# Two blocks of a transformer on one core: where the state-space Gelu and the poles' setup stand in the program

## The chip, the cores and the metric

The kernel runs on one core of a Trainium2 chip. The metric is the device time of one launch in microseconds. A core has TensorE (PE; its weight loads are PEld), VectorE (DVE), ScalarE (ACT), GpSimd (POOL) and the queue engine SyncE (SP). Each works through its own queue in the order in which the program puts the instructions there.

## The reference

x is 512 tokens of 1024 values, all in float32. The first block runs two layers of

```python
x = x + 0.5 * swiglu(rmsnorm(x, g_ffn1[l]), w_ffn1_gate[l], w_ffn1_up[l], w_ffn1_down[l])
...
x = x + merged @ w_out[l]
x = x + 0.5 * swiglu(rmsnorm(x, g_ffn2[l]), w_ffn2_gate[l], w_ffn2_up[l], w_ffn2_down[l])
```

The second block has an even layer (stick-breaking attention of 8 heads beside a state-space mixer) and an odd one (gated linear attention). What the change touches is the even layer:

```python
q = rms_norm(q.reshape(bsz, L, SB_HEADS, SB_HEAD_DIM), sb_q_norm_g[i])
k = rms_norm(k.reshape(bsz, L, SB_HEADS, SB_HEAD_DIM), sb_k_norm_g[i])
o_a = stick_breaking_attention(q, k, v).reshape(bsz, L, SB_WIDTH) * jax.nn.silu(z_a)
o_b = s5_mixer(u, ...) * jax.nn.silu(z_b)
```

`s5_mixer` makes complex poles and input weights from its parameters (`lam_bar = exp(lam * dt)`, `b_bar = (lam_bar - 1) / lam * b`), scans over time, and ends with `y = gelu(y)` and a gate `y * sigmoid(y @ w_glu + b_glu)`.

## The kernel before

Every large product is three matmuls (`mm3`, lines 200 to 202): both operands are split into a high and a low part. ScalarE copies the high part of a weight chunk (tile `wh`, line 111), VectorE subtracts to get the low part (`wl`, line 112). Two buffers each of `wr`, `wh` and `wl` hold the chunks, so a split waits until PE is done with the chunk before the last. A pool of 32 wide buffers (`g`) holds most intermediates, 8 PSUM banks (`b`) the products. The program is written in one order, and a scheduler places the instructions on each engine's queue at build time; what it chose is fixed.

The even layer (`even`, from line 1357) works in rounds c = 0 to 4. In a round below 4, PE makes q, k and v of heads 2c and 2c+1 in halves of two token tiles (`qk_half`, `form_b_pair`). ScalarE copies each half out of PSUM with the token scale `rce` and squares it; after the second half, VectorE, GpSimd (a power) and VectorE again make the norm's scale and multiply q or k (line 247); PE then turns them by transposes (`qk_turn`, line 269). Beside that, a round takes the two heads of the round before through `logits` (three banks; on ScalarE copies, Abs, Exp, Ln; on VectorE a maximum; on GpSimd a triangular mask, line 1259), `sums` (running sums by matmuls with constant triangles, lines 205), `values` and `gated`, with a unit of z by `silu_unit` for each. `ha` is the first of these heads, `hb` the second.

The state-space part runs one quarter of its groups a round: `states(c)` (matmuls 64 wide, a scan on VectorE), `outputs(c)` (matmuls into one bank, a copy by ScalarE, a store `s_ys` by SP's queue), `fed` and `load` (SP's queue fetches the next quarter's inputs `s_us` and tables), and `finish(c - 1)`: eight loads of the stored outputs by SP's queue, then the Gelu, which is an addition on VectorE, a Square on ScalarE, two operations on VectorE, a Tanh on ScalarE and two more on VectorE. Before the change `finish` stands behind `logits(ha)`.

A feed-forward (`ffn`, line 365) goes through its hidden units in thirds of 8, 8 and 6 chunks; each third ends with a down projection of four columns. The list `extra` hangs a step behind each of the first six half columns of every third's down projection. In the first feed-forward of layer 0 the poles' setup (`s5_setup`, some 60 short operations on VectorE, a chain of powers on GpSimd, two loads of b by ScalarE's queue) hangs in the last third, and `s5_keep`, which stores three results by GpSimd's queue, on the step behind it.

Of the kernel before, what the change touches and what calls it, by code (L numbers as in the profile page):

```python
# [50 lines left out]
class Kern:  # L51
# [851 lines left out]
    def s5_setup(self):  # L903

        nc, ins = self.nc, self.ins
# [3 lines left out]
        def A(n, w=16):  # L909
            i = 1 if n in ("s5th", "s5kk", "s5t2") else 0 if n in ("s5cn", "s5sn") else 2  # L910
            if i == 2:
                return self.tiny(w)
            used[i] += w
            return (keep, work)[i][:, used[i] - w:used[i]]
# [18 lines left out]
        t2, s, c = A("s5t2", W), A("s5s", W), A("s5c", W)  # L933
# [14 lines left out]
        nr, ni, t, u, den = A("s5nr"), A("s5ni"), A("s5t"), A("s5u"), A("s5den")  # L948
# [13 lines left out]
        self.tt(u, nr, im, ALU.mult)  # L962
        self.tt(t, t, u, ALU.subtract)
        self.tt(ci, t, den, ALU.mult)
        br, bi, t1, t2 = self.g()[:, 0:256], self.g()[:, 0:256], self.g()[:, 0:256], self.g()[:, 0:256]
        nc.scalar.dma_start(br, ins["s5_b_re"])
        nc.scalar.dma_start(bi, ins["s5_b_im"])
        v = lambda a: a.rearrange("p (j c) -> p j c", c=16)
        wide = lambda a: a.rearrange("p (j c) -> p j c", c=1).to_broadcast([P, 16, 16])
        both = self.g()  # L970
# [16 lines left out]
        for n in (1, 2, 4):  # L987
            a, b = slice(1, n + 1), slice(n + 1, 2 * n + 1)
            cr, ci = (t[:, n:n + 1, :].to_broadcast([P, n, 16]) for t in (lr, li))
            t = self.g()  # L990
            t1, t2 = (t[:, i * 64:i * 64 + n * 16].rearrange("p (k j) -> p k j", j=16) for i in range(2))
# [359 lines left out]
    def even(self):  # L1351
        nc, ins = self.nc, self.ins
        w_in = ins["even_w_in"]
        gf = self.par["g_final"]
        gg = self.const([P, KD], "gg")
        self.tt(gg, gf, self.par["even_norm_g_2"], ALU.mult)

        us, ys, oa, heads, sz = [], [], [], {}, {}
        load, feed, fed, states, outputs, finish = self.s5_steps(us, ys)
        xs = self.norm_start(gg)  # L1360
        w = self.weights(w_in[16])
        acc, acc2 = self.squares(), self.squares(gf)
        b = [self.form_a(w, 0, xs), self.form_a(w, 1, xs)]
        r1 = self.rms(self.col_sums(acc), 4, D, EPS)
        w = self.weights(w_in[17])
        b.append(self.form_a(w, 0, xs))
        ssf = self.tiny(4)
        self.tt(ssf, self.col_sums(acc2), r1, ALU.mult)
        self.tt(ssf, ssf, r1, ALU.mult)
        rcol = self.const([P, 4], "rce")  # L1370
        self.tt(rcol, self.rms(ssf, 4, D, EPS), r1, ALU.mult)
        b.append(self.form_a(w, 1, xs))
        d1, d2 = self.diag(r1), self.diag(rcol)
        R, R1 = self.rows(rcol, d2), self.rows(r1, d1)
        for i in range(4):
            u = self.g()
            self.tt(u, b[i], R, ALU.mult)
            us.append(u)
            feed(i)
        fed(0)  # L1380
        load(0)
        logits, sums, values, gated = self.sb_steps(heads, oa)

        def silu_unit(w, j):
            b = self.form_a(w, j, xs)
            s = self.g()
            self.tt(s, b, R, ALU.mult)
            self.act(s, s, AF.Silu)
            return s

        ob_s = []
        for c in range(5):
            ha, hb, hp = 2 * c - 2, 2 * c - 1, 2 * c - 3
            q, k = {}, {}
            if c < 4:
                w = self.weights(w_in[c])
                self.qk_half(w, 0, xs, rcol, q)
            else:
                wz = self.weights(w_in[18])
                ob_s.append(silu_unit(wz, 0))  # L1400
            if c > 1:
                values(hp)
                gated(hp, sz.pop(hp))
            if c > 0:
                logits(ha)
                finish(c - 1)
            if c < 4:
                self.qk_half(w, 2, xs, rcol, q)
                w = self.weights(w_in[4 + c])
                self.qk_half(w, 0, xs, rcol, k)  # L1410
                states(c)
            else:
                ob_s.append(silu_unit(wz, 1))
                wz = self.weights(w_in[19])
                ob_s.append(silu_unit(wz, 0))
                yp = [self.split(y) for y in ys]
            if 0 < c < 4:
                with self.tc.issue_after(q["rms"].ins):
                    sums(ha)
            elif c > 0:  # L1420
                sums(ha)
            if c < 4:
                self.qk_half(w, 2, xs, rcol, k)
                w = self.weights(w_in[8 + c])
                v2 = [self.g(), self.g()]
                qT = self.qk_turn(q, self.par["sb_q_norm_g_2"], P ** -0.5)
                self.form_b_pair(w, 0, xs, rcol, lambda i: v2[0][:, i * 256:(i + 1) * 256])
            else:
                ob_s.append(silu_unit(wz, 1))
            if c > 0:  # L1430
                values(ha)
            if c < 4:
                self.form_b_pair(w, 2, xs, rcol, lambda i: v2[1][:, i * 256:(i + 1) * 256])
                kT = self.qk_turn(k, self.par["sb_k_norm_g_2"], 1.0)
                for i in range(2):
                    heads[2 * c + i] = (qT[i], kT[i], [v2[t // 2][:, (t % 2) * 256 + i * P:(t % 2) * 256 + (i + 1) * P]
                                                       for t in range(4)])
            if c > 0:
                logits(hb)
                wz = self.weights(w_in[12 + c - 1])  # L1440
                sz[ha] = silu_unit(wz, 0)
                gated(ha, sz.pop(ha))
            if c < 4:
                outputs(c)
                if c < 3:
                    fed(c + 1)
                    load(c + 1)
            if c > 0:
                sz[hb] = silu_unit(wz, 1)
                if c < 4:  # L1450
                    sums(hb)
            if c == 1:
                for k in range(KD):
                    self.stt(self.x[k], self.x[k], gf[:, k:k + 1], R1, ALU.mult, ALU.mult)
        ob = []
        os_ = [self.split(o) for o in oa[:4]]
        for c in range(2):
            w = self.weights(ins["s5_w_glu"][c])
            for j in range(2):
                n = 2 * c + j  # L1460
                b = self.form_a(w, j, yp)
                th = self.g()
                self.act(th, b, AF.Tanh, scale=0.5, bias=self.bglu[:, n:n + 1])
                self.stt(th, th, 1.0, ys[n], ALU.add, ALU.mult)
                self.stt(th, th, 0.5, ob_s[n], ALU.mult, ALU.mult)
                ob.append(self.split(th, *(self.sp.tile([P, S], F32R, tag=t, name=self.nm(t), bufs=KD) for t in ("xh", "xl"))))
        os_ += [self.split(o) for o in oa[4:]] + [None] + ob
        banks, ws = [], {}

        def part(n, ks, first, last):  # L1470
            if n % 2 == 0 and first:
                ws[n // 2] = [self.weights(ins["even_w_out"][n // 2], k, 6) for k in (6, 0)][::-1]
            if first:
                banks.append(self.bank())
            js = slice((n % 2) * P, (n % 2 + 1) * P)
            for k in ks:
                w = ws[n // 2][k // 6]
                self.mm3(banks[n], (w[0][:, k % 6, js], w[1][:, k % 6, js]), os_[k], first and k == ks[0],
                         last and k == ks[-1])

        sums(7)
        ks = [8, 9, 10, 11, 0, 1, 2, 3, 4, 5, 6]
        part(0, ks, True, False)
        values(7)
        gated(7, sz.pop(7))
        os_[7] = self.split(oa[7])
        part(1, ks, True, False)
        for n in range(KD):
            part(n, [7] if n < 2 else ks + [7], n >= 2, True)
            self.tt(self.x[n], banks[n], self.x[n], ALU.add)  # L1490
# [222 lines left out]
def build(tc, ins, out, upto=99, first=0):  # L1713
    with ExitStack() as ctx:
        K = Kern(ctx, tc, ins, out)
        K.setup()
        idle = [nothing] * 6
        extras = [[[K.bias_loads, K.biases] + idle[2:] + idle + [K.s5_setup, K.s5_keep],
                   idle + K.s5_quad(0) + K.s5_quad(1)],
                  [idle + K.s5_quad(2) + K.s5_quad(3), idle + K.s5_tables(0) + [nothing] + K.s5_tables(1)]]  # L1720
        for l in range(DEPTH if first == 0 else 0):
# [120 lines left out]
```

## Time and profile before

| | us |
|---|---|
| median of three runs | 3108.08 (3104.66 to 3109.74) |
| the profiled execution | 3108.96 |
| its span, first to last instruction | 3107.1 |
| PE busy | 3044.2 |
| VectorE busy | 2039.7 |
| ScalarE busy | 1354.2 |
| GpSimd busy | 166.8 |

Times in the rows are microseconds from the span's start. A line ("L269") is that of the kernel; where a helper issues an operation, the line is the helper's and the tiles tell which step it is. PEclk is the granted share of TensorE's full clock: 1 is 2.4 GHz, half of it 1.2 GHz. The rounds of the even layer lie between about 2450 and 2810, the first feed-forward between 0 and 363.

### The profile page before, as it was taken

The numbers are of one execution on the slowest core, as the hardware profiler recorded it, in microseconds if no ns is written. First come the engines' busy times: TensorE is split into PE (matmuls) and PEld (weight loads), VectorE is DVE, ScalarE is ACT, GpSimd is POOL, SyncE is SP. The second block draws the span as 40 slices with busy tenths as digits, with TensorE's granted clock in tenths as the row PEclk, the third lists the DMA queues.
The fourth block names the chain that finished last, engine by engine and source line by source line (L and its number), as shares of the span: only waits on it lengthen the run. The fifth ranks groups of instructions, "written<-read, shape, count | busy, mean of one in ns | idle before, by whom it ended". The sixth has DMA issues, their size and how long they took to land. (4 is left out here: it accounts for less than half of the span.)

```text
span 3107.1 us, 44082 instructions
## 1 busy us (share of the span) xinstructions
PE 3044.2 (98%) x17718; PEld 2653.8 (85%) x17718; DVE 2039.7 (66%) x3630; ACT 1354.2 (44%) x2351; POOL 166.8 (5%) x308
## 2 busy tenths in 40 slices
PE   9999999999999999999999999999999988899999
PEld 7898888889888988898989889888989977777887
DVE  7787845655667887888864655558878644454643
ACT  5343335543443434443434553344434455463532
POOL 1000200000000011001010000000000010010010
PEclk9999999999999999999999999999999998899999
DMA  4332333322222333323343322222233331212211
GB/s 152 101 109 91 117 106 115 112 83 82 98 92 96 111 116 123 107 95 120 104 141 106 114 92 82 95 95 96 96 117 102 131 116 59 71 63 69 105 68 55
DMA packets 73548, 311.13 MB, mean 100 GB/s; under 512 B 18836, under 2 KB 20820, under 8 KB 44800
## 3 DMA queue, kind: packets, MB, share of 16 engines
q1 hardware_dynamic: 59680, 282.39, 26.4%
q10 hardware_dynamic: 9584, 16.74, 1.9%
q0 software_dynamic: 4080, 9.20, 1.2%
q8 instruction: 139, 2.28, 0.3%
q14 instruction: 65, 0.53, 0.1%
HBM read 292.48 MB, written 12.66 MB: 98 GB/s over the span
## 5 line engine op out<-in xcount | busy, mean ns | idle before, releaser
L200 PE MATMUL b<-xh,wh 128*128 128x512 f32 (+1 forms) x1880 | 693.7, 369 | 7.4 <-ACT xh L253 6.7
L202 PE MATMUL b<-xh,wl 128*128 128x512 f32 (+1 forms) x1880 | 684.4, 364 | 4.0 <-DVE wl L112 3.6
L201 PE MATMUL b<-xl,wh 128*128 128x512 f32 (+1 forms) x1880 | 683.8, 364 | 1.3 <-DVE xl L97 1.3
L111 ACT ACTIVATE wh<-wr 128x1024 fp32r<-128x1024 f32 (+2 forms) x396 | 383.0, 1004 | 582.8 <-PE b L201 347.7
L112 DVE TENSOR_TENSOR wl<-wr,wh 128x1024 fp32r<-128x1024 f32 (+2 forms) x396 | 453.1, 1162 | 154.7 <-ACT wh L111 152.9
L202 PE MATMUL b<-g,wl 128*128 128x512 f32 x1168 | 461.6, 395 | 1.2 <-DVE wl L112 1.2
L200 PE MATMUL b<-g,wh 128*128 128x512 f32 x1168 | 462.8, 396 | 0.0
L201 PE MATMUL b<-g,wh 128*128 128x512 f32 x1168 | 461.1, 395 | 1.5 <-DVE g L97 1.5
L200 PEld LDWEIGHTS b<-xh,wh 128*128 128x128 f32 x1880 | 356.5, 190 | 62.8 <-ACT xh L253 6.7
L202 PEld LDWEIGHTS b<-xh,wl 128*128 128x128 f32 x1880 | 356.1, 189 | 61.3 <-DVE wl L112 4.7
L201 PEld LDWEIGHTS b<-xl,wh 128*128 128x128 f32 x1880 | 356.4, 190 | 57.4 <-issue 2.1
L243 DVE TENSOR_TENSOR g<-b,g 128x512 f32<-128x512 f32 (+2 forms) x265 | 183.9, 699 | 254.0 <-PE b L202 238.9
L202 PEld LDWEIGHTS b<-g,wl 128*128 128x128 f32 x1168 | 220.0, 188 | 52.9 <-DVE wl L112 1.6
L201 PEld LDWEIGHTS b<-g,wh 128*128 128x128 f32 x1168 | 220.0, 188 | 52.5 <-DVE g L97 2.3
L200 PEld LDWEIGHTS b<-g,wh 128*128 128x128 f32 x1168 | 220.2, 189 | 52.0 <-issue 2.0
L200 PE MATMUL b<-wh,xh 128*128 128x256 f32 x896 | 259.5, 290 | 0.0
L201 PE MATMUL b<-wl,xh 128*128 128x256 f32 x896 | 256.4, 286 | 1.1 <-DVE wl L112 1.1
L202 PE MATMUL b<-wh,xl 128*128 128x256 f32 x896 | 255.7, 285 | 0.0
L243 DVE TENSOR_TENSOR g<-g,g 128x512 f32<-128x512 f32 (+8 forms) x373 | 201.8, 570 | 66.8 <-ACT g L253 62.4
L243 DVE TENSOR_TENSOR g<-g,b 128x256 f32<-128x256 f32 (+1 forms) x484 | 177.0, 397 | 29.1 <-PE b L202 25.2
L96 ACT ACTIVATE sw<-s 128x512 fp32r<-128x512 f32 x180 | 111.8, 630 | 191.9 <-DVE s L243 158.5
L253 ACT ACTIVATE g<-g 128x512 f32<-128x512 f32 (+4 forms) x280 | 143.6, 528 | 102.3 <-DVE g L243 86.1
(240 smaller groups left out, 5114.3 us busy)
## 6 DMA issues: line engine op xcount, KB each, us to landing
wr<-in_w_ffn_up SPq DMA_DIRECT2D x44, 1024.0 KB, 4.8
wr<-in_w_ffn_gate SPq DMA_DIRECT2D x43, 1024.0 KB, 4.8
wr<-in_w_ffn_down SPq DMA_DIRECT2D x32, 1024.0 KB, 4.9
wr<-in_w_gate SPq DMA_DIRECT2D x24, 1024.0 KB, 4.8
wr<-in_w_in SPq DMA_DIRECT2D x20, 1024.0 KB, 4.8
wr<-in_even_w_in SPq DMA_DIRECT2D x20, 1024.0 KB, 5.0
wr<-in_w_ffn_down SPq DMA_DIRECT2D x16, 768.0 KB, 4.2
g<-tb ACTq DMA_DIRECT2D x48, 256.0 KB, 3.0
```

The lines of the kernel that those rows point to most:

```text
L96: self.nc.scalar.activation(hi, src, AF.Copy)
L111: nc.scalar.activation(hi[:, :, js], raw[:, :, js], AF.Copy)
L112: nc.vector.tensor_tensor(out=lo[:, :, js], in0=raw[:, :, js], in1=hi.bitcast(F32)[:, :, js], op=ALU.subtract)
L200: t.matmul(out, l[0], r[0], start=start, stop=False)
L201: t.matmul(out, l[0], r[1], start=False, stop=False)
L202: t.matmul(out, l[1], r[0], start=False, stop=stop)
L243: return (eng or self.nc.vector).tensor_tensor(out=out, in0=a, in1=b, op=op)
L253: self.nc.scalar.activation(out, a, f, **kw)
```

## The change

It moves `finish(c - 1)` in rounds 1 to 3 from behind `logits(ha)` to the end of the round, behind `gated(ha)` and ahead of `outputs(c)`; in round 4 it stays. It moves `s5_setup` and `s5_keep` from the last third of the first feed-forward to the middle third, with one empty step between them. The loads of b go by GpSimd's queue, and four half-used wide buffers become two.

```diff
--- before.py
+++ after.py
@@ -962,9 +962,9 @@
         self.tt(u, nr, im, ALU.mult)
         self.tt(t, t, u, ALU.subtract)
         self.tt(ci, t, den, ALU.mult)
-        br, bi, t1, t2 = self.g()[:, 0:256], self.g()[:, 0:256], self.g()[:, 0:256], self.g()[:, 0:256]
-        nc.scalar.dma_start(br, ins["s5_b_re"])
-        nc.scalar.dma_start(bi, ins["s5_b_im"])
+        (br, bi), (t1, t2) = ((t[:, 0:256], t[:, 256:512]) for t in (self.g(), self.g()))
+        nc.gpsimd.dma_start(br, ins["s5_b_re"])
+        nc.gpsimd.dma_start(bi, ins["s5_b_im"])
         v = lambda a: a.rearrange("p (j c) -> p j c", c=16)
         wide = lambda a: a.rearrange("p (j c) -> p j c", c=1).to_broadcast([P, 16, 16])
         both = self.g()
@@ -1403,7 +1403,8 @@
                 gated(hp, sz.pop(hp))
             if c > 0:
                 logits(ha)
-                finish(c - 1)
+                if c == 4:
+                    finish(3)
             if c < 4:
                 self.qk_half(w, 2, xs, rcol, q)
                 w = self.weights(w_in[4 + c])
@@ -1440,6 +1441,8 @@
                 wz = self.weights(w_in[12 + c - 1])
                 sz[ha] = silu_unit(wz, 0)
                 gated(ha, sz.pop(ha))
+            if 0 < c < 4:
+                finish(c - 1)
             if c < 4:
                 outputs(c)
                 if c < 3:
@@ -1715,7 +1718,7 @@
         K = Kern(ctx, tc, ins, out)
         K.setup()
         idle = [nothing] * 6
-        extras = [[[K.bias_loads, K.biases] + idle[2:] + idle + [K.s5_setup, K.s5_keep],
+        extras = [[[K.bias_loads, K.biases] + idle[2:] + [K.s5_setup, nothing, K.s5_keep],
                    idle + K.s5_quad(0) + K.s5_quad(1)],
                   [idle + K.s5_quad(2) + K.s5_quad(3), idle + K.s5_tables(0) + [nothing] + K.s5_tables(1)]]
         for l in range(DEPTH if first == 0 else 0):
```

Three places in ScalarE's queue show what the scheduler makes of it. In the rows, `sb` tiles of 1280 columns are the logits' work buffers, `g<-b,rce` copies half of q, k or v out of PSUM, `g,y<-g` squares it, `wh<-wr` splits a weight chunk, and a `g<-g` of 512 columns is a Square, Tanh or Silu.

Round 1, from the two copies behind the mask on. Before:

```order
L253 ACTIVATE g_23508<-sb_23495 128x128
L253 ACTIVATE g_23507<-sb_23495 128x128
L111 ACTIVATE wh_23975<-wr_23973 128x8x128 x2
L253 ACTIVATE g_23523<-g_23522 128x512
L253 ACT_TABLE_LOAD
L253 ACTIVATE g_23524<-g_23523 128x512
L253 ACTIVATE g_23429<-b_23533,rce 128x256 x2
L253 ACTIVATE g_23532,y_23430<-g_23429 128x128 x4
L253 ACTIVATE g_23608<-b_23612,rce 128x256 x2
L253 ACTIVATE g_23611,y_23610<-g_23608 128x128 x4
```

Now:

```order
L253 ACTIVATE g_23506<-sb_23493 128x128
L253 ACTIVATE g_23505<-sb_23493 128x128
L253 ACTIVATE g_23427<-b_23512,rce 128x256 x2
L253 ACTIVATE g_23511,y_23428<-g_23427 128x128 x4
L253 ACTIVATE g_23587<-b_23591,rce 128x256 x2
L253 ACTIVATE g_23590,y_23589<-g_23587 128x128 x4
L253 ACT_TABLE_LOAD
L253 ACTIVATE sb_23492<-sb_23492 128x1280
L111 ACTIVATE wh_23954<-wr_23952 128x8x128
L253 ACTIVATE g_23588<-b_23712,rce 128x256 x2
L253 ACTIVATE g_23711,y_23589<-g_23588 128x128 x4
L111 ACTIVATE wh_23954<-wr_23952 128x8x128
```

The weight split (of z's chunk), Square, table load and Tanh stood ahead of the copies of q's second half and k's first; now those copies follow at once, the Exp of the sums behind them, and the split comes in two halves around the copies of k's second half.

The end of round 1 and the start of round 2, before; the first row copies the state outputs out of PSUM:

```order
L253 ACTIVATE g_24027<-b_24010 128x512
L253 ACT_TABLE_LOAD
L253 ACTIVATE g_24006<-g_24006 128x512
L111 ACTIVATE wh_24309<-wr_24307 128x8x128 x2
L253 ACT_TABLE_LOAD
L253 ACTIVATE sb_23954<-sb_23954 128x1280
L253 ACTIVATE sb_24201<-b_24194 128x512
L253 ACTIVATE sb_24201<-b_24196 128x256
L253 ACTIVATE sb_24201<-b_24195 128x512
L253 ACTIVATE g_24042<-s_r_3452 128x4x63 x2
L253 ACT_TABLE_LOAD
L253 ACTIVATE g_24082<-g_24082 128x512
```

Now, from the table load ahead of the Exp of the sums of `hb`:

```order
L253 ACT_TABLE_LOAD
L253 ACTIVATE sb_23933<-sb_23933 128x1280
L253 ACTIVATE g_23999<-g_23998 128x512
L253 ACTIVATE g_24000<-g_23999 128x512
L253 ACTIVATE g_24025<-b_24008 128x512
L253 ACTIVATE sb_24199<-b_24192 128x512
L253 ACTIVATE sb_24199<-b_24194 128x256
L253 ACTIVATE sb_24199<-b_24193 128x512
L253 ACTIVATE sb_24200<-sb_24199 128x1280
L253 ACTIVATE sb_24200<-sb_24200 128x1280
L253 ACT_TABLE_LOAD
L253 ACTIVATE sb_24200<-sb_24200 128x1280
```

Square, Tanh and the copy of the state outputs now stand behind that Exp and ahead of the logits' three copies, and the logits' Abs, Exp, table load and Ln follow these without other work between them.

Round 4, from the Exp of the sums on. Before:

```order
L253 ACTIVATE sb_25360<-sb_25360 128x1280
L253 ACT_TABLE_LOAD
L253 ACTIVATE g_25523<-g_25523 128x512
L253 ACTIVATE sb_25541<-b_25534 128x512
L253 ACTIVATE sb_25541<-b_25536 128x256
L253 ACTIVATE sb_25541<-b_25535 128x512
L253 ACTIVATE sb_25542<-sb_25541 128x1280
L253 ACT_TABLE_LOAD
L253 ACTIVATE sb_25542<-sb_25542 128x1280
L253 ACT_TABLE_LOAD
L253 ACTIVATE sb_25542<-sb_25542 128x1280
L111 ACTIVATE wh_25748<-wr_25746 128x8x128 x2
```

Now, from the copy of the state outputs, which has Exp, Square and Tanh ahead of it:

```order
L253 ACTIVATE g_25431<-b_25414 128x512
L253 ACTIVATE sb_25539<-b_25532 128x512
L253 ACT_TABLE_LOAD
L253 ACTIVATE g_25459<-g_25459 128x512
L253 ACTIVATE g_25521<-g_25521 128x512
L253 ACTIVATE sb_25539<-b_25533 128x512
L253 ACTIVATE sb_25539<-b_25534 128x256
L253 ACTIVATE sb_25540<-sb_25539 128x1280
L253 ACT_TABLE_LOAD
L253 ACTIVATE sb_25540<-sb_25540 128x1280
L111 ACTIVATE wh_25746<-wr_25744 128x8x128
L253 ACT_TABLE_LOAD
```

A table load and two Silus have moved in between the first and the second copy of the logits, and half of a weight split ahead of the last table load.

## Rows read from the trace of the kernel before

**Rows 1.** the page's first line and, from its part 2, the clock line in 40 slices

```profile
span 3107.1 us, 44082 instructions
...
PEclk9999999999999999999999999999999998899999
```

**Rows 2.** waits of TensorE: waiting engine, tile, line <- releaser: us in total, times, longest

```profile
PE b L269 <- DVE g L247: 34.0, 3, 11.3
...
PE b L205 <- POOL sb L1259: 5.5, 2, 2.8
PE b L202 <- DVE wl L112: 4.8, 2, 3.6
```

**Rows 3.** stretches from PE's return: busy us of PE, PEld, DVE, ACT, POOL; clock, DMA, GB/s

```profile
366.60:376.60 10.00, 9.98 (x38) 8.22 (x39) 9.49 (x11) 3.88 (x8) 2.64 (x4) 0.85 0.80 274
2521.40:2531.40 10.00, 9.96 (x58) 9.04 (x59) 9.28 (x25) 3.65 (x13) 1.83 (x6) 0.73 0.00 0
2585.20:2595.20 10.00, 9.98 (x56) 8.05 (x57) 2.43 (x5) 0.51 (x2) 0.70 (x3) 0.85 0.25 64
2607.50:2617.50 10.00, 9.98 (x59) 8.90 (x60) 9.26 (x25) 4.00 (x13) 1.83 (x6) 0.77 0.01 2
2670.90:2680.90 10.00, 9.95 (x43) 7.41 (x44) 2.43 (x5) 0.51 (x2) 0.73 (x3) 0.70 0.24 66
2694.70:2704.70 10.00, 9.97 (x57) 9.20 (x58) 9.27 (x25) 3.31 (x12) 1.83 (x6) 0.69 0.01 2
```

**Rows 4.** time line of ScalarE, round 1: start, us, engine, line, operation, shapes, count [idle before <-releaser]

```profile
2501.24 0.50 ACT L253 ACTIVATE g<-sb 128x128 f32<-128x128 f32 x2
2510.12 2.00 ACT L111 ACTIVATE wh<-wr 128x1024 fp32r<-128x1024 f32 x2 [8.38 <-PE b L202]
2514.65 0.63 ACT L253 ACTIVATE g<-g 128x512 f32<-128x512 f32 x1 [2.53 <-DVE g L250]
2515.30 1.28 ACT L253 ACT_TABLE_LOAD   x1
...
2517.13 0.82 ACT L253 ACTIVATE g<-b,rce 128x256 f32<-128x256 f32 x2
```

**Rows 5.** time line of VectorE, same stretch

```profile
2503.07 0.69 DVE L243 TENSOR_TENSOR sb<-b,sb 128x512 f32<-128x512 f32 x1 [1.07 <-PE b L205]
...
2511.21 2.36 DVE L112 TENSOR_TENSOR wl<-wr,wh 128x1024 fp32r<-128x1024 f32 x2 [6.04 <-ACT wh L111]
...
2519.14 0.17 DVE L247 TENSOR_SCALAR y<-y 128x8 f32<-128x8 f32 x1 [0.73 <-ACT g L253]
2521.07 1.81 DVE L247 TENSOR_SCALAR g<-g,y 128x128 f32<-128x128 f32 x8 [1.77 <-POOL y L243]
```

**Rows 6.** time line of ScalarE, end of round 1 and round 2

```profile
2561.70 1.27 ACT L253 ACTIVATE sb<-sb 128x1280 f32<-128x1280 f32 x1 [2.23 <-POOL sb L1259]
2568.61 0.60 ACT L253 ACTIVATE sb<-b 128x512 f32<-128x512 f32 x1 [5.65 <-PE b L205]
...
2581.95 1.27 ACT L253 ACTIVATE sb<-sb 128x1280 f32<-128x1280 f32 x1
```

**Rows 7.** time line of TensorE, state matmuls of round 2

```profile
2581.31 1.15 PE L205 MATMUL b<-g,g 128*64 128x64 f32 x32
```

**Rows 8.** time line of ScalarE, round 4

```profile
2749.12 1.27 ACT L253 ACTIVATE sb<-sb 128x1280 f32<-128x1280 f32 x1
...
2753.73 0.51 ACT L253 ACTIVATE g<-sb 128x128 f32<-128x128 f32 x2 [1.44 <-POOL sb L1259]
```

**Rows 9.** stretches of the middle third, the last third and the rounds, columns as Rows 3

```profile
232.00:267.00 35.00, 35.00 (x153) 28.43 (x153) 21.96 (x30) 7.91 (x10) 0.00 (x0) 1.00 0.25 90
336.20:352.50 16.30, 16.30 (x72) 13.18 (x71) 15.68 (x63) 3.89 (x5) 4.75 (x17) 1.00 0.40 138
2485.00:2735.00 250.00, 209.90 (x1382) 182.70 (x1381) 109.84 (x202) 127.72 (x250) 26.80 (x63) 0.90 0.25 82
```

**Rows 10.** issues of SP's queue, round 1

```profile
2551.85 3.28 SPq L1181 DMA_DIRECT2D g<-s_us  x7
```

## The prediction

> **What bounds the kernel now.** I read the page's span and clock line first, then the waits of TensorE, then the time lines of one of those waits on four engines. The page gives a span of 3107.1 us and a PE clock line that is 9 in all slices but two, near the end [rows 1]. So nearly all of the time is matrix work at full rate, which the change does not touch, and what can be won are the places where PE stands, and the lower clock behind them. The waits name them: three waits of the transposes (L269) for VectorE's scaling, 34.0 us together; two of the running sums for GpSimd's mask, 5.5 us; one of 3.6 us (of a group of 4.8 us) for a low weight part [rows 2]. Behind each, the ten microseconds that start with PE's return show a mean clock below 1, where PE is busy all the time: 0.73, 0.77 and 0.69 behind the three long ones, 0.85 and 0.70 behind the two of the mask, 0.85 behind the single one [rows 3]. A tenth below 1 over 10 us is 1 us of full-rate work that was not done.
>
> The long wait in round 1 is told by ScalarE. After the copies that end at 2501.7 it stands 8.38 us at the weight split wh, until PE has finished the second half of k at 2510.1. Only then come the split (2.00), a wait of 2.53 for VectorE, the Gelu's Square, its table load (1.28), its Tanh, and at 2517.1 the copies of q's second half out of PSUM, whose squares give q's norm [rows 4]. VectorE does the low weight parts (2.36) and the Gelu's first three operations before the norm's first step at 2519.1, then waits 1.77 for GpSimd's power, and scales q from 2521.1 [rows 5]. PE turns q at 2521.4. The matmuls whose result ScalarE fetches at 2517.1 were done before those of k: the order of ScalarE's queue makes the wait, not the work.
>
> **The change part by part.**
>
> *Gelu out of the way, rounds 1 to 3.* In the changed order the copies of q's and k's halves stand right behind the copies that end at 2501.7, and wh, Square and Tanh behind them. Two pairs of copies (0.82 each) [rows 4] with four squares each (1.2, what lies between the copies and 2519.1 [rows 5]) are over some 4 us after 2501.7; q's norm needs only the first half of that, and with 0.17, 1.77 and 1.81 for the scaling [rows 5] q is ready at about 2507.6, before PE is done with k at 2510.1. In round 1 the wait goes whole. In rounds 2 and 3 VectorE has two sums (0.69 each [rows 5]) ahead of the norm that are fed by matmuls now standing inside k's second half; sums, norm and power take 3.3 us, of which the rest of that half covers a part. The bounds of what stays are 0 and 3.3 us a round; I take 1.5, twice, between them, as PE still has about a third of that half to do. Gain: 34.0 for the waits, and 2.7 + 2.3 + 3.1 = 8.1 for the clock behind them; loss 3.0.
>
> *The mask's chain in rounds 2 and 3.* Before, the logits' copies at 2568.6 are followed by a table load, a Silu, q's copies and squares and two weight splits, strewn among the chain's Abs, Exp and Ln; the Ln starts at 2581.95 [rows 6]. PE has passed the state matmuls (2581.31 to 2582.5 [rows 7]) and waits. In the changed order the chain runs without any of these: two and a bit copies, Abs, Exp, one table load, Ln, which at 1.27 to 1.28 each ends some 7 us after 2568.6 instead of 14.6 us. The mask is then ready long before PE asks. What comes ahead of the chain instead is the Gelu: Square, Tanh and the copy of the state outputs, about 0.63 each [rows 4], and VectorE's two operations between; the Exp ahead of them ends at 2563.0 [rows 6], so all are over by about 2566.5, 2 us before the logits' first copy. The eight loads of the Gelu's input are moved as well, in SP's queue behind three loads of weights instead of ahead of them, and are wanted later by more than half a round. Cost nothing while that holds; if that cover is gone, the copy comes late by what is missing. Gain 5.5, and 1.5 + 3.0 = 4.5 for the clock.
>
> *Round 4.* Here the changed order puts a table load and two Silus between the first and the second of the logits' copies, and half a weight split ahead of the Ln: 1.28 + 2 x 0.63 + 1.00 = 3.5 us later than before. Before, the Ln starts at 2749.12 and the mask lets ScalarE go on at 2753.7 [rows 8], which is also when PE asks for it, so there is no slack. The bounds are 0 and 3.5 us; I take 3.2, and 1.5 of clock, the smallest that stands behind a wait in [rows 3]. Loss 4.7. ScalarE's table load takes 1.28 us here and the next instruction starts 0.01 us later [rows 4]; the Trainium skill (ScalarE: Activation LUTs, What ACT_TABLE_LOAD costs) counts 2.66 us for a switch, with a drain. By that rule round 4 would lose 1.4 us more and the total be 3060; the trace does not bear it out. The three table loads that fall away in the whole program are off the path otherwise.
>
> *The poles' setup.* It leaves the last third of the first feed-forward, where VectorE is busy for 15.7 of 16.3 us [rows 9] and falls behind until PE waits 3.6 us for a low weight part [rows 2], with 1.5 of clock behind it [rows 3]. In the middle third VectorE has 35.0 - 22.0 = 13.0 us free between 232 and 267 [rows 9]. The setup is at most those 15.7 us, and the low weight parts and updates of x in that stretch are not its own, so it fits or nearly. The wait goes (5.1 us) and none comes; the bounds are 0 and 5.1. The two loads of b go from ScalarE's queue to GpSimd's, where they, the powers and the three stores of what is kept meet nothing: GpSimd is busy 0.00 us there [rows 9]. VectorE asks for b only near the end of the setup. Cost nothing; if that cover were gone, VectorE would stand for the landing, behind it the down projection's updates, which PE outruns only when its 8 banks are full.
>
> **The sum.** 34.0 + 8.1 - 3.0 + 5.5 + 4.5 - 4.7 + 5.1 = 49.5 us. The profiled execution took 3108.96 us (3107.1 and what lies around it), 0.9 above the median of the three runs; from the median of 3108.08 this gives **3059 us**.
>
> **The rivals.**
>
> *The scale stays exposed.* ScalarE could still reach q's copies only when k is done, as where PSUM banks or buffers hold it up. Then copies, squares, norm, power and the first scaling, 0.8 + 1.2 + 0.2 + 1.8 + 0.2 = 4.2 us, stay in each of three rounds, with 1.5 of clock each: 3 x 5.7 = 17.1, less the 3.0 already counted: 3073 us. For it: VectorE and GpSimd are in the same chain. Against it: the rows of the changed order above.
>
> *The middle third pays.* If VectorE's backlog there meets the next third's weights, the 5.1 us come back: 3064. For it: if all 15.7 us are the setup's, 2.7 do not fit. Against it: PE ran through both ends of that stretch without a wait.
>
> *Slower: the state outputs' copy holds up the queue of the loads.* The copy now stands behind Exp, Square and Tanh, at about 2566.5 instead of before 2551.5, and in SP's queue its store is followed by the loads of the next round's inputs, seven of which take 3.28 us to issue [rows 10], then by tables and weights. PE's next state matmuls come at 2581.3 [rows 7]. Store, seven loads and landing end at about 2576, an estimate that allows for the store and for the landing what the seven take to issue each: 5 us to spare. It decides only when the copy comes over 5 us later still, and the run is slower than before only when each of three rounds then loses 49.5 / 3 = 16.5 us, so when the copy is 21 us late: about 3115. Against it: nothing that the Tanh needs comes that late.
>
> *The half clock counts in full.* Over 2485 to 2735 the mean clock is 0.90 [rows 9], so 25 us of full-rate work; I counted 12.6, since for the rest PE stood anyway and a slow clock cost nothing. The Trainium skill (TensorE: Matmul & The Clock Gate, Terms) takes the penalty as the throttled time times the missing share, whatever PE did. By that the gain is 12.4 larger: 3047. The rows behind each wait, where PE is busy, speak against it.
>
> *No change.* If ScalarE's order were not what holds PE, but the transfers, all waits would stay: 3108, or 3103 with the feed-forward's. In [rows 4] the named releaser is PE itself, which speaks against it.
>
> **How the numbers follow.** Forecast 0.72, scale exposed 0.11, middle third 0.08, full clock 0.04, no change 0.03, slower 0.02. The range holds the forecast with its bounds (7.7 less where rounds 2 to 4 lose nothing; 3.6 more at the upper bound of rounds 2 and 3), the middle third, the full clock and the exposed scale: 3046 to 3076. A measurement of this kernel tells about 0.2%, 6.2 us, from no change. All but the last two are faster by more: faster 0.95, same 0.03, slower 0.02.
>
> **What would show it.** Right: no L269 wait over 4 us among PE's waits, no 8 us stand of ScalarE at wh before q's copies, both waits for GpSimd's mask gone, a new one of about 3 us near the fourth round, no wait near 363, clock line at 9 in the two slices. Wrong: the three waits at 4 to 6 us (scale exposed), a new wait near 270 (middle third), PE waiting at the 64-wide state matmuls for loads (slower).

## The result, and the profile after

The changed kernel takes **3057.89 us** (median of four runs, 3056.54 to 3058.85) beside 3108.91 (3104.66 to 3110.2) for the kernel before on the same chip: ratio 0.9838, interval 0.9821 to 0.9855. The profiled execution took 3056.54 us. Of its page, the first line, the total of TensorE and the clock line, which answer to [rows 1]:

```profile
span 3054.8 us, 44104 instructions
...
PE 3032.2 (99%) x17718; PEld 2643.2 (87%) x17718; DVE 2037.9 (67%) x3630; ACT 1349.8 (44%) x2348; POOL 176.4 (6%) x310
...
PEclk9999999999999999999999999999999999999999
```

The two slices below 9 are gone. The span is 52.3 us shorter, and the page says where from. Before, PE was busy for 3044.2 of 3107.1 us, so it stood for 62.9; now it stands for 3054.8 - 3032.2 = 22.6. So 40.3 us are waits that went, and 12.0 us are the same 17718 matmuls in less busy time, which is the clock. The waits of TensorE in the changed kernel, to be held against [rows 2]:

```profile
PE b L200 <- ACT xh L253: 7.2, 1, 7.2
PE b L269 <- DVE g L247: 2.9, 2, 1.4
PE b L205 <- POOL sb L1259: 1.9, 1, 1.9
```

The first is the start of the program, 6.7 us before. The 34.0 us of the transposes are 2.9, the 5.5 of the mask in rounds 2 and 3 are gone, a wait of 1.9 for the mask has come in round 4, and the wait near 363 is gone. ScalarE in round 1, time line of the changed kernel, where [rows 4] had the long stand at wh:

```profile
2495.66 0.50 ACT L253 ACTIVATE g<-sb 128x128 f32<-128x128 f32 x2
2496.05 0.82 ACT L253 ACTIVATE g<-b,rce 128x256 f32<-128x256 f32 x2
...
2507.03 1.04 ACT L111 ACTIVATE wh<-wr 128x1024 fp32r<-128x1024 f32 x1
```

The copies of q's second half follow the mask's copies at once; the split of z's chunk comes at 2507.0, when PE has left k (at 2504.3), and does not wait for it. VectorE scales q from 2500.0, and PE turns it at 2504.3 without a wait.

In round 2 the logits' chain runs as in the changed order. Its first copy and its Ln:

```profile
2548.88 0.60 ACT L253 ACTIVATE sb<-b 128x512 f32<-128x512 f32 x1 [1.86 <-PE b L205]
...
2554.75 1.27 ACT L253 ACTIVATE sb<-sb 128x1280 f32<-128x1280 f32 x1
```

They are 5.9 us apart, and the chain is over after 7.1, where [rows 6] had the Ln 13.3 us behind the copy. What round 2 keeps is on VectorE:

```profile
2570.25 1.29 DVE L243 TENSOR_TENSOR sb<-b,sb 128x512 f32<-128x512 f32 x2 [3.04 <-PE b L205]
2571.46 0.16 DVE L247 TENSOR_SCALAR y<-y 128x8 f32<-128x8 f32 x1
2573.37 1.89 DVE L247 TENSOR_SCALAR g<-g,y 128x128 f32<-128x128 f32 x8 [1.75 <-POOL y L243]
```

The additions of the running sums wait 3.04 us for PE with the norm's first step behind them; PE asks for q at 2572.5 and gets it 1.43 us later. Round 3 shows the same. Round 4, ScalarE:

```profile
2690.13 0.60 ACT L253 ACTIVATE sb<-b 128x512 f32<-128x512 f32 x1 [1.55 <-PE b L205]
2690.75 1.28 ACT L253 ACT_TABLE_LOAD   x1
2692.04 1.15 ACT L253 ACTIVATE g<-g 128x512 f32<-128x512 f32 x2
2693.10 0.85 ACT L253 ACTIVATE sb<-b 128x512 f32<-128x512 f32 x2
...
2697.75 1.04 ACT L111 ACTIVATE wh<-wr 128x1024 fp32r<-128x1024 f32 x1
2698.81 1.28 ACT L253 ACT_TABLE_LOAD   x1
2700.11 1.27 ACT L253 ACTIVATE sb<-sb 128x1280 f32<-128x1280 f32 x1
```

From the first copy to the Ln it is 9.98 us. Before, the copies stood here:

```profile
2741.97 0.60 ACT L253 ACTIVATE sb<-b 128x512 f32<-128x512 f32 x1 [1.66 <-PE b L205]
2743.04 0.88 ACT L253 ACTIVATE sb<-b 128x256 f32<-128x256 f32 x2 [0.48 <-PE b L205]
```

To the Ln at 2749.12 [rows 8] that was 7.15 us, so the inserted work makes the Ln 2.83 us late.

### The profile page after: what moved, and what is told of

Same layout as the page of the kernel before. It is cut to its first block, busy times and chain, and to the rows that moved or that the text cites. A ratio compares the mean times of both kernels' runs of the same rounds, so it can differ in the third digit from the quotient of the medians.

```text
span 3054.8 us, 44104 instructions
## 1 busy us (share of the span) xinstructions
PE 3032.2 (99%) x17718; PEld 2643.2 (87%) x17718; DVE 2037.9 (67%) x3630; ACT 1349.8 (44%) x2348; POOL 176.4 (6%) x310
## 4 chain that ended last, share of the span: by engine, by line
PE 94%; ACT 2%; issue 1%; DVE 1%; POOL 1%; DMA 0%; SPq 0%; POOLq 0%; ACTq 0%; DVEq 0%
PE b L200 29%; PE b L202 29%; PE b L201 29%; PE b L205 7%; PE b L269 2%; ACT g L253 1%; ACT sb L253 1%; ACT L253 1%; POOL sb L1259 0%; DVE wl L112 0%; POOL y L243 0%; DMA g<-s_kst 0%; DVE sb L250 0%; DMA wr<-in_w_ffn_gate 0%; DMA g<-tb 0%
## 5 line engine op out<-in xcount | busy, mean ns | idle before, releaser
L200 PEld LDWEIGHTS b<-xh,wh 128*128 128x128 f32 x1880 | 355.5, 189 | 62.9 <-ACT xh L253 7.2
```

The costliest lines, as they stand in the source:

```text
L200: t.matmul(out, l[0], r[0], start=start, stop=False)
```

## The experiments

Ratios are to the kernel before, measured on the same chip in the same set of runs.

### The two parts alone

**gelu_alone** is the change without its setup part, **setup_alone** the change without its Gelu part.

> Only the move of the Gelu (rounds 1 to 3, round 4 as in the change); the setup and its loads as before. Theory, from the terms of the prediction: everything but the 5.1 us of the first feed-forward is here, so 44.4 us below the kernel before, about 3064; the long waits of the transposes and the mask's waits gone, the wait of 3.6 us near 363 still there with a stretch at half clock behind it. Rival: the two parts share a cause (the wait near 363 shifts what comes later), then the gain is the full 50 or under 40.

> Only the setup in the middle third, with its loads by GpSimd's queue and two wide buffers; the Gelu as before. Theory: 5.1 us (3.6 of wait, 1.5 of clock) below the kernel before, about 3103, no wait near 363 and none near 267, the three waits of 11.3 us untouched. Rival one: the middle third pays, PE waits for a low weight part near 267 and the time is that of the kernel before. Rival two: the wait only passes on to the next thirds, then also no gain.

Measured: 3064.40 us (ratio 0.9858, 0.9844 to 0.9871) and 3102.28 us (0.9975, 0.9965 to 0.9984), against 3109.22 before. So 44.8 us, against 44.4 expected, and 6.9 us, against 5.1. They add to 51.7; the change as a whole brought 51.0. The interval of setup_alone reaches from 5.0 to 10.9 us, so its 6.9 cannot be told from 5.1: its nine runs fall into two groups, 3097.8 to 3098.9 and 3102.3 to 3104.5 us. Its profiled execution is of the first group. In it 3.6 us of PE's waits are gone, those near 363, and PE is busy for 7.0 us less, of which 1.5 belongs to the stretch near 363. Most of the rest is the clock behind waits that this edit does not touch: behind the two for the mask it was 1.00 and 0.85 instead of 0.85 and 0.70. The first kernel's waits of TensorE still hold the feed-forward's, the second's still the three of the transposes and those of the mask:

```profile
PE b L202 <- DVE wl L112: 4.8, 2, 3.6
PE b L269 <- DVE g L247: 2.9, 2, 1.4
```

```profile
PE b L269 <- DVE g L247: 34.0, 3, 11.4
...
PE b L205 <- POOL sb L1259: 5.5, 2, 2.8
```

### What holds q

Two things stood ahead of q's copies in ScalarE's queue: the split of z's chunk and the Gelu. **gelu_left_out** takes the Gelu's work away and leaves the split:

```diff
-            self.act(t, y, AF.Square)
...
-            self.stt(y, th, 1.0, t, ALU.add, ALU.mult)
             ys.append(y)
```

> The kernel before with the Gelu's own operations left out (the addition stays; the state-space outputs enter their gate without the Gelu), nothing moved. In ScalarE's queue the split of z's chunk still stands ahead of the copies of q's second half, with no Square, table load or Tanh between them. Theory (the split's wait for the end of k is what holds q): three waits of the transposes stay at 6 to 7 us each (11.3 less Square, Tanh, table load and the wait of 2.53 for VectorE, about 5), still with half clock behind them; about 15 us below the kernel before from these, with the clock 15 to 20. Rival (the Gelu's work holds q, the split is beside the point): waits of at most 1.5 us, 40 us or more below the kernel before.

**split_held** is the reverse. It holds the split behind q's last square, with `st["sq"]` set to that instruction, and leaves the Gelu in its place:

```diff
...
-                wz = self.weights(w_in[12 + c - 1])
+                if c < 4:
+                    with self.tc.issue_after(q["sq"].ins):
+                        wz = self.weights(w_in[12 + c - 1])
+                else:
+                    wz = self.weights(w_in[12 + c - 1])
```

> The kernel before with one thing held back: the split of z's chunk may not stand in ScalarE's queue ahead of the squares of q's second half (rounds 1 to 3). The Gelu stays where it was, so Square, table load and Tanh still stand ahead of q's copies. Theory, after the first runs: 11.35 us are two things in series, the split's wait with its 2.00 and the 2.53 behind it, and the Gelu's chain of Square, two operations of VectorE and Tanh. Without the split VectorE is free for the Gelu's addition at 2505.2, so Square, VectorE and Tanh end near 2508.9, q's copies, squares, norm and first scaling near 2513.1, against PE's request at 2510.1: waits of about 3 us in each of three rounds instead of 11.3, 25 us less and some 4 of clock, about 29 us below the kernel before, 3080. Rival one (the split is all): waits of under 1.5 us, about 3068. Rival two, as in the move by the least: the wait turns up at the transposes of k, about 3093.

Measured: 3092.58 us (0.9948, 0.9933 to 0.9963), 16.6 us below before where 15 to 20 were expected, and 3083.61 us (0.9916, 0.9901 to 0.9931). The waits of the transposes, first with the Gelu left out, then with the split held:

```profile
PE b L269 <- DVE g L247: 20.2, 3, 6.7
```

```profile
PE b L269 <- DVE g L247: 9.4, 5, 3.0
```

It is 6.7 us a round without the Gelu and 3.0 without the split in the way (the group of five holds two short waits more). Neither alone brings the wait to nothing, and neither rival holds. In the second kernel VectorE shows the series that was reckoned with:

```profile
2506.11 1.22 DVE L250 SCALAR_TENSOR_TENSOR g<-g,par,g 128x512 f32<-128x512 f32 x1
...
2511.85 0.17 DVE L247 TENSOR_SCALAR y<-y 128x8 f32<-128x8 f32 x1 [0.73 <-ACT g L253]
2513.79 1.81 DVE L247 TENSOR_SCALAR g<-g,y 128x128 f32<-128x128 f32 x8 [1.76 <-POOL y L243]
```

The Gelu's addition starts once the sums are done, the norm after the Gelu, and PE, which asked at 2511.1, has q at 2514.1. Where 29 us below before were expected, 26.6 came.

**gelu_behind_q** moves the Gelu by the least, behind q's second half instead of the end of the round:

```diff
-                finish(c - 1)
+                if c == 4:
+                    finish(3)
             if c < 4:
                 self.qk_half(w, 2, xs, rcol, q)
+                if c > 0:
+                    finish(c - 1)
                 w = self.weights(w_in[4 + c])
```

> The Gelu moved by the least: only behind the second half of q, in rounds 1 to 3; setup as before. In ScalarE's queue the copies of q's second half then stand at once behind the mask's copies, split, Square and Tanh behind them, as in the change; but a table load, a Silu, copies of q and weight splits still stand strewn between the logits' copies and the Ln, as before. Theory: the three long waits go (at most 1.5 us each), the two waits of about 2.75 us for GpSimd's mask stay with their clock, and so does that near 363: 34.0 + 8.1 - 3.0 = 39 us below the kernel before, about 3069. Rival: the end of the round is not needed, the mask's waits go too, about 3064 like the move to the end of the round.

Measured: 3093.90 us (0.9951, 0.9939 to 0.9964), 15.3 us below before where 39 were expected. This theory was wrong for the transposes; the two waits for the mask stayed as expected. There are still three waits of the transposes, and ScalarE's time line of round 1 says which they are:

```profile
PE b L269 <- DVE g L247: 19.0, 3, 6.3
...
PE b L205 <- POOL sb L1259: 5.8, 2, 2.9
```

```profile
2515.94 0.63 ACT L253 ACTIVATE g<-g 128x512 f32<-128x512 f32 x1 [2.61 <-DVE g L250]
2517.79 0.63 ACT L253 ACTIVATE g<-g 128x512 f32<-128x512 f32 x1 [1.22 <-DVE g L243]
2518.32 0.82 ACT L253 ACTIVATE g<-b,rce 128x256 f32<-128x256 f32 x2
...
2525.85 2.00 ACT L111 ACTIVATE wh<-wr 128x1024 fp32r<-128x1024 f32 x2 [5.54 <-PE b L202]
2527.76 0.82 ACT L253 ACTIVATE g<-b,rce 128x256 f32<-128x256 f32 x2
```

q is in time now (PE turns it at 2511.1). But the Gelu has pushed k's copies back, and the next split, that of the next round's q chunk, stands at 2525.9 for the end of v, ahead of the copies of k's second half, which PE finished at 2511.1. PE waits 6.32 us at the turn of k. So the wait is not tied to q: in both orders the half that was still uncopied when a split came up in the queue waited for that split's buffer. At the end of the round the Gelu has no half behind it that PE wants soon; that place, and not the mere getting out of q's way, is what most of the change is worth. Against gelu_alone this run keeps 16.1 us more of the transposes' waits and 3.9 more of those for the mask.

### The poles' setup

**old_loads** is the changed kernel with the loads of b on ScalarE's queue and four wide buffers again (that hunk of the diff undone). **setup_longer** and **setup_much_longer** are the changed kernel with the setup's polynomials computed three and six times over, **last_third_longer** the kernel before with them computed twice:

```diff
-        for acc, co in ((s, cs), (c, cc)):
+        for acc, co in ((s, cs), (c, cc)) * 3:
```

> The changed kernel with the two loads of b on ScalarE's queue and four wide buffers again; the setup stays in the middle third. Theory (the loads and buffers are covered and cost nothing there): 3058, no wait of PE between 200 and 400. Rival (ScalarE's queue or the buffers stand in the way of the next weights): a wait of PE near 240 to 270, 2 us or more above the changed kernel.

> The changed kernel with the polynomials of the setup computed three times over (28 more operations of 144 columns on VectorE at about 0.31 us, 8.6 us), all in the middle third of the first feed-forward. In the changed kernel VectorE has 3.8 us free between 232 and 267. Theory (room on VectorE is the cover of the setup there): 8.6 - 3.8 = 4.8 us do not fit, and PE waits for some part of that behind 260 for a low weight part, 2 to 5 us with a stretch of half clock: 2 to 7 us above the changed kernel's 3058. Rival (PE's banks and VectorE's lead into the next third take it up): no wait, 3058.

> The kernel before with the polynomials of the setup computed twice (14 more operations, 4.3 us of VectorE) in the last third of the first feed-forward. Theory: behind this third the next stage needs all of x at once, so VectorE's lag is exposed one for one: the wait near 363 grows from 3.6 to 7.9 us. Rival (the wait of 3.6 has another cause): it stays at 3.6 to 4.

> The changed kernel with the polynomials of the setup six times over in the middle third (70 more operations, some 21.7 us of VectorE; three times over showed no wait). Between 232 and 363 VectorE of the changed kernel is busy for 109.9 of 131 us, so 21.1 us are free in all. Theory: no wait as long as the lag can be made good before the next layer asks for x at 363 and no weight split is late; 21.7 us is about the edge of the first and over the lead of the splits: waits of PE of 1 to 8 us between 260 and 365. Rival (lag is free there whatever its size): none.

Measured: old_loads 3056.94 us (0.9831, 0.9814 to 0.9847), no wait there: loads and buffers make no difference that these runs can tell. setup_longer 3057.66 us (0.9831, 0.9817 to 0.9846), no wait between 200 and 400: the theory fell. The operations took less than was reckoned. Two of the six series in the time line of setup_much_longer:

```profile
239.62 2.70 DVE L250 SCALAR_TENSOR_TENSOR y<-y,g 128x144 f32<-128x144 f32 x12
...
242.53 2.71 DVE L250 SCALAR_TENSOR_TENSOR y<-y,g 128x144 f32<-128x144 f32 x12
```

A series of 14 operations thus comes 2.91 us after the one before it. The two more of setup_longer, in its time line just as far apart, are 5.8 us and not 8.6, still more than the 3.8 us of room. (The page's total rose by only 4.0, from 2037.9 to 2041.9.) Six times over, it is five series more, 14.6 us (2050.0 in the page, 12.1 more), and the kernel took 3056.54 us in one run, with these waits between 220 and 400:

```profile
PE b L202 <- DVE wl L112: 1.3, 2, 0.8
```

In the last third one series more, 2.9 us, gave 3113.1 us in one run and, where 7.9 us of wait were expected,

```profile
PE b L202 <- DVE wl L112: 7.4, 1, 7.4
```

So 2.9 us more of VectorE cost 3.8 us of wait in the last third (7.4 instead of 3.6); 14.6 us cost 1.3 in the middle one. The room in the third itself does not explain that; the rows that follow point to what stands behind it. VectorE of the kernel before at the wait near 363:

```profile
364.09 0.67 DVE L243 TENSOR_TENSOR x<-x,g 128x512 f32<-128x512 f32 x1
364.69 0.73 DVE L250 SCALAR_TENSOR_TENSOR xl<-x,par,xh 128x512 fp32r<-128x512 f32 x1
365.36 1.21 DVE L112 TENSOR_TENSOR wl<-wr,wh 128x1024 fp32r<-128x1024 f32 x1
```

These are the last update of x, its low part and then the weight's low part: the next stage starts from all of x, so the lag is PE's. Behind the middle third come matmuls that use the old x, which is read from the program, and the lag is made good later, which the trace of setup_much_longer shows. VectorE is there busy for 34.1 of 35 us from 232 to 267, for 32.5 of 33 to 300 and for 19.6 of 20 to 320; the next stretch (columns as [rows 3]) is still fuller than the 11.06 us of the changed kernel:

```profile
320.00:336.00 16.00, 16.00 (x113) 14.92 (x113) 15.05 (x29) 7.50 (x12) 0.00 (x0) 1.00 0.33 102
```

From 336 to 352 it is 12.24 us against 12.87 in the changed kernel, so the lag is gone before x is asked for near 363. last_third_longer and setup_much_longer are single runs.

### What is left, and a faster version

**q_first** holds the additions of the sums behind q's scalings, with `st["scaled"]` set to the last of these; **round4** holds two Silus (of the tiles in `late`) and the gate that needs one behind the Ln of round 4's first logits; **both** has the two edits together:

```diff
-                with self.tc.issue_after(q["rms"].ins):
+                with self.tc.issue_after(q["rms"].ins), self.tc.issue_after(q["scaled"].ins):
                     sums(ha)
...
                 if c == 4:
+                    with self.tc.issue_after(sb["ln"].ins):
+                        for s in late:
+                            self.act(s, s, AF.Silu)
+                    gated(hp, sz.pop(hp))
                     finish(3)
...
```

> The changed kernel with VectorE's three additions of the running sums held behind the scalings of q in rounds 1 to 3 (nothing else). Theory: the 1.43 us that PE still waits in rounds 2 and 3 for q are these additions, which wait for matmuls inside k's second half and stand ahead of the norm; behind the scalings they cost nothing, since the Exp that follows has about 4 us before PE asks for its values: both waits of 1.43 go, with the stretch of 3.41 us at half clock behind the second (1.7): 4.6 us below the changed kernel, about 3053. Rival: the Exp is late instead and PE waits for it at the values, 3058 or more.

> The changed kernel with two Silus (the last unit of z, the first of round 4) held behind the Ln of round 4's first logits, and the gate that needs the first of them behind it. Theory: the 1.94 us that PE waits for the mask in round 4 are the table load and the two Silus between the copies (1.28 + 1.15) and the half weight split ahead of the Ln (1.04): without them the Ln ends 3.5 us earlier, the wait goes, and the half clock that such a wait has had behind it (1.7): 2 to 3.6 us below the changed kernel, 3054 to 3056. Rival: the Silus come late for what follows, and the wait turns up behind round 4: 3058.

> The last two edits together on the changed kernel. Theory: their gains are at different places and add, 4.6 + 3.6 = 8.2 us: about 3050, faster than both kernels. Rival: one of them only moves PE's waits to the tail behind round 4 (2728 to 2752 in the changed kernel), 3053 to 3056.

Measured: 3051.89 us (0.9817, 0.9804 to 0.983), 3052.22 us (0.9822, 0.9809 to 0.9836; runs from 3051.57 to 3057.6) and 3049.49 us (0.9809, 0.9796 to 0.9823; runs from 3048.88 to 3050.01). In q_first the norm's first step is at 2567.46, the additions come behind the scalings, and PE turns q without a wait:

```profile
2567.46 0.17 DVE L247 TENSOR_SCALAR y<-y 128x8 f32<-128x8 f32 x1 [1.67 <-ACT g L253]
2569.39 1.66 DVE L247 TENSOR_SCALAR g<-g,y 128x128 f32<-128x128 f32 x8 [1.75 <-POOL y L243]
...
2572.61 0.69 DVE L243 TENSOR_TENSOR sb<-b,sb 128x512 f32<-128x512 f32 x1
```

In round4 the Ln starts 5.9 us behind the first copy (2689.00 to 2694.88) instead of 9.98, and the wait for the mask is gone. The edits gained 6.0 and 5.7 us on the changed kernel's median, where 4.6 and at most 3.6 were expected. In round4's profiled execution PE waits 2.8 us less and is busy for 3030.1 instead of 3032.2 us; that second part is the clock, behind the wait of round 3 among others, which the edit does not touch. Both edits together are the fastest version here, 8.4 us below the changed kernel, about the 8.2 expected but less than the two gains added. A part of each gain is the clock behind small waits, which comes and goes from execution to execution (last section). In the profiled execution of both, moreover, one wait of the transposes between 1500 and 2000, far from either edit, takes 2.3 us, where the longest of its group is 0.7 in q_first and 0.5 in round4; its cause was not looked into.

## Why the prediction was right

The forecast was 3059 us, the result 3057.9. Step by step:

- **The long waits of rounds 1 to 3.** 34.0 less 3.0 was forecast, 34.0 less 2.9 came, with the round and the cause as named: none in round 1, 1.43 in rounds 2 and 3 where 1.5 was taken, from VectorE's additions ahead of the norm, which q_first shows. The rival of the exposed scale had 4.2 us in each round and is out.
- **The mask in rounds 2 and 3.** 5.5 forecast, both waits gone; the chain is over 7.1 us after its first copy where "some 7" stood. No run took the strewn work out of the chain by itself, so that this is what held the mask is read from the two time lines. The Gelu's own work is not: with it left out the two waits were still 4.5 us, 2.2 each.
- **Round 4.** Mis-sized: 4.7 forecast, 1.94 of wait measured, with the clock at full rate behind it in the profiled execution. The Ln comes 2.83 us later instead of 3.5, since the 0.48 us for which the second copy waited for PE are now covered and the two Silus take 1.15. And PE needs less of the mask than ScalarE does: in the changed kernel it goes on 1.21 us behind the mask's start (2703.03 to 2704.24), ScalarE's copies 1.68 behind it. Before, the mask started at 2752.05 and PE asked only at 2754.00, so there were 0.7 us of slack. A wait of 0.86 behind it, for VectorE, went as well. The step that failed is "there is no slack". The Trainium skill (ScalarE: Activation LUTs, What ACT_TABLE_LOAD costs) would have made it 1.4 us worse with its 2.66 us for a switch. The trace disagrees on the drain: the load took 1.28 us, and the whole delay of 2.83 leaves no room for more.
- **The setup.** 5.1 forecast, 6.9 by setup_alone, from which 5.1 cannot be told. The wait of 3.6 went and none came. VectorE of the changed kernel in the middle third, beside [rows 9]:

```profile
232.00:267.00 35.00, 35.00 (x153) 28.42 (x152) 31.23 (x86) 7.91 (x10) 10.78 (x25) 1.00 0.30 107
```

It is busy 31.2 instead of 22.0 us, so the setup takes about 9.3 us there and not up to 15.7. That it fits was right, but the reason was not the one that counts: 14.6 us more still cost only 1.3 there.

- **The clock.** 8.1 + 4.5 - 1.5 + 1.5 = 12.6 forecast from the rows behind each wait; PE's busy time fell by 12.0. That they agree so closely is in part luck: the 1.5 counted behind round 4's wait did not come, 1.7 that was not counted came behind round 3's, and setup_alone shows how much of such a sum changes without a change in the waits. The rival in which the half clock counts in full had 25. That count is the one of the Trainium skill (TensorE: Matmul & The Clock Gate, Terms), the throttled time by the missing share; this trace disagrees. Stretches of round 1 in the kernel before (us, then busy time of PE, PEld, DVE, ACT, POOL, then the clock) show why it is out:

```profile
2510.08:2513.13 3.05, 0.00 (x1) 0.00 (x0) 1.92 (x2) 2.00 (x2) 0.00 (x0) 1.00 0.00 0
2513.13:2521.43 8.30, 0.00 (x0) 0.00 (x1) 4.25 (x9) 6.31 (x23) 2.03 (x3) 0.50 0.35 128
2521.43:2526.78 5.35, 5.34 (x24) 4.73 (x25) 5.25 (x16) 3.16 (x11) 0.69 (x5) 0.50 0.00 0
2526.78:2532.00 5.22, 5.22 (x38) 4.61 (x38) 4.05 (x11) 0.84 (x2) 1.63 (x1) 1.00 0.00 0
```

Of 13.65 us at half clock (1.2 GHz) PE stood for 8.30 and worked for 5.35, which cost 2.7.

- **The slower rival.** The store of the state outputs is issued at 2547.04, the seven loads behind it are out by 2550.7, and the state matmuls of round 2 start at 2561.57 without a wait. No run delayed the copy on purpose, so the point at which this would bite was not tried. The prediction's 3115 for it follows from none of its terms: with the copy 21 us late they give the time of the kernel before.

By the sum, waits of 34.0 - 3.0 + 5.5 - 3.2 + 3.6 = 36.9 us were to go, and 40.3 went: round 4 was 1.3 better, and of 2.9 us of shorter waits for VectorE in the rounds and behind them 2.7 went too, which the prediction had not looked at; a few of 0.5 came. With the clock the profiled execution's span is 52.3 us shorter where 49.5 were forecast, the medians are 51.0 apart. So the time was right because the large terms were. Of the terms taken between bounds, the 1.5 us a round for q was met (1.43), which is in part luck, since it was an estimate between 0 and 3.3; round 4 was taken 2.8 us too high, with its clock; and the clock as a whole came 0.6 short.

## What to carry to other kernels

When an engine stands at an instruction that waits for a buffer, look at what is queued behind it and has been ready for long: here copies stood 15 us (2501.7 to 2517.1) behind a weight split and what followed it. Moving one piece of work out of the way helps only if the new place has nothing urgent behind it; the least move brought 15 us, the end of the round 45. And when work is to be put on an engine, look not only at how much room the engine has there, but at whether the stage behind asks at once for all that it produces: here 2.9 us cost 3.8 where it does, and 14.6 cost 1.3 where it does not.

## What the runs showed of the hardware that was not expected

The clock behind a short wait is not settled by the wait's length. In the changed kernel the ten microseconds behind the wait of round 2 (1.43 us), of round 3 (1.43) and of round 4 (1.94) read:

```profile
2573.90:2583.90 10.00, 9.90 (x71) 8.76 (x72) 9.16 (x25) 5.90 (x15) 1.74 (x4) 1.00 0.01 2
2643.94:2653.94 10.00, 9.90 (x60) 8.91 (x61) 9.16 (x25) 5.90 (x15) 1.74 (x4) 0.83 0.01 2
2704.24:2714.24 10.00, 10.00 (x40) 7.25 (x41) 2.60 (x6) 3.90 (x6) 1.80 (x7) 1.00 0.18 52
```

Two equal waits, one with the clock at full rate behind it and one with 0.83. From execution to execution it changes too: round 3's wait of 1.43 had 1.00 behind it in gelu_alone, old_loads, round4 and both runs with a longer setup, and round 4's wait of 1.9 had 0.83 in gelu_alone. The kernel before had 0.85 and 0.70 behind its two waits of 2.75, setup_alone 1.00 and 0.85 behind the same waits. The split_held kernel's three waits of 3.0 us had 0.83 behind each, and those of 6.7 us with the Gelu left out 0.75, 0.70 and 0.84. So a term of 1.5 us for each short wait, as the prediction had for round 4, is right on some executions only.

Short operations of VectorE overlap: a single one of 144 columns shows 0.30 to 0.31 us, but 12 of them in two independent chains take 2.70 us together, so that the next starts about 0.22 us after the one before. Five series of 14 more took 14.6 us of its queue, 0.21 an operation, while the page's total of busy time rose by 12.1; the time line, not the total, gives the dose.
